# A one-core encoder block with 32 routed experts: how the first expert gets its rows, and when the half blocks add their lower part

## The chip, the cores and the metric

One core of one Trainium2 chip runs the whole layer in one launch. The metric is device time in microseconds (us), the median of several executions. Names: PE is the tensor engine, ACT the scalar engine, DVE the vector engine, POOL the GpSimd engine, SP the engine that here only issues DMAs.

## The reference

One layer over 1024 tokens of width 1024: a token mixer, a layer norm, a mixture of experts, a second layer norm. What matters here is the mixture; each token takes 2 of 32 experts, and each expert has three matrices of 2 MB.

```
x = layer_norm(ALPHA * x + mix, ln1_g, ln1_b)
gl = xf @ w_rg + b_rg                       # 4 groups, top 1
el = (xf @ w_re + b_re).reshape(T, 4, 8)    # 8 experts in the group, top 2
weights = (g_w[:, None] * top_v).reshape(-1)
hb = silu(xb @ w_gate[e]) * (xb @ w_up[e])  # per block of rows of one expert
yb = hb @ w_down[e]
y  = segment_sum(yb * row_w[:, None], row_tok)
x  = layer_norm(ALPHA * x + y, ln2_g, ln2_b)
```

The counts per expert are known only at run time.

## The kernel before, in words

**Numbers.** Every product is made of two-part splits: ACT copies a tile rounded (`hi`), DVE subtracts it from the tile (`lo`), and PE adds three products (`mm3`, lines 95 to 98). For expert weights this is `w_split`, lines 1005 to 1014: tiles `we` (raw), `weh` and `wel`.

**The end of the mixer.** A loop over 8 tiles of 128 tokens makes the output projection (`out_proj`, tiles `z`), `residual(i)` (DVE: sum, statistics), `r_transposed` and `logits` (PE), `route_a` (DVE: top 1 and top 2, one-hot rows `ahot`), `norm1` (ACT, then POOL in two passes, lines 844 and 845) and `store1`, which writes the normed rows to `x1d` in HBM. `rank` counts on PE how many earlier tokens chose each expert; `route_b` makes of it each token's place in a table `tabd` in HBM and scatters (token, weight) there with two indirect DMAs from POOL (line 939). Tile 7 comes last and alone.

**The start of the experts.** SP reads back the table's rows of the four first experts (`slots`, line 1082), and POOL gathers the rows of `x1d` that they name (`gather`, line 1193, tile `xin`). The first four experts (`FIXED`) are taken in their own order, the other 28 by falling count: lines 1085 to 1104 rank them on DVE with 28 x 28 comparisons on every partition and write `perm`, from which SP reads each expert's number.

**The expert stage.** An expert is six chunks of 1 MB: gate 0 and 1, up 2 and 3, down 4 and 5. `SEQ` has the order: chunks 0 to 3 of a block, then chunks 4 and 5 of the block before. SP issues the loads (`load_to`) as far ahead as 20 tiles in rotation allow; ACT and DVE split three chunks ahead (`AHEAD`); SP's queue also reads each later block's table rows (`place`, line 1188, tile `psl`, eight in rotation). Each block ends in an indirect DMA that adds its rows to `accd` in HBM (`finish`, line 1289).

**Half blocks.** Eleven of the 33 blocks have 64 rows (`few_rows`). They put both parts of the rows side by side, so PE needs two products in place of three; the second half of the partitions must then be added to the first. ACT copies it out (`low_part`, `low_y`, tiles `low` and `lowy`), and PE adds it with a product by the identity (`add_low`, line 1178). In the loop at line 1329 the gate's lower part is added after chunk 2, the down product's after the next chunk, which is the next block's chunk 0.

**Overflow.** `overflow_setup` (line 1117) works out which rows did not fit; some 30 DVE instructions at block 21.

Of the kernel before, what the change touches and what calls it, by code (L numbers as in the profile page):

```python
# [11 lines left out]
F32 = mybir.dt.float32  # L12
# [9 lines left out]
S = 1024  # L22
# [27 lines left out]
def kernel(  # L50
# [726 lines left out]
    lgc = rp_.tile([128, 2, 36], F32, name="lgc")  # L777
    wg = rp_.tile([128, KT, 36], F32, name="wg")

    def logit_setup():  # L780
# [75 lines left out]
    def store_acc(i):  # L856
        sp.dma_start(accd[i * 128:(i + 1) * 128], ACC[i])
# [19 lines left out]
    def route_a(i):  # L877
# [31 lines left out]
        a = rp_.tile([128, 2, NG, EPG], F32, name="ah", bufs=2)  # L909
# [10 lines left out]
    def rank(i):  # L920
# [5 lines left out]
        pe.matmul(rk, tri[:, 0, :], ahot[:, i, :], start=False, stop=True)  # L926
        RT[i] = rk, RT[i]

    def route_b(i):
        rk, av = RT[i]  # L930
        idf = rp_.tile([128, 2], F32, name="idf")
# [3 lines left out]
        idx = rp_.tile([128, 2], I32, name="idx", bufs=4)  # L935
        dve.tensor_copy(idx, idf)
        for c in range(2):
            pool.memset(spacer, 0.0)
            st = pool.indirect_dma_start(
                out=tabd, out_offset=bass.IndirectOffsetOnAxis(ap=idx[:, c:c + 1], axis=0),  # L940
                in_=pay[:, i, c, :], in_offset=None)
# [4 lines left out]
    SCAT = []  # L946
    spacer = rp_.tile([1, 1], F32, name="spacer")

# [84 lines left out]
    for i in range(NT):  # L1033
        if i + 1 < NT:
            load_xr(i + 1)
        load_to({0: 6, 2: 7, 5: 8, 6: 9, 7: 11}.get(i, 0))
        ka, kb = (K0, K0) if i == 0 else (2, 4) if i + 1 < NT else KLAST
        out_proj(i, 0, ka)
        if i:
            r_transposed(i - 1)  # L1040
        if i + 1 < NT:
            m_split(i + 1)
        if i > 1:
            store1(i - 2)
            scale_acc(i - 2)
            store_acc(i - 2)
        out_proj(i, ka, kb)
        if i:
            logits(i - 1)
            route_a(i - 1)  # L1050
        if i:
            norm1(i - 1)
        out_proj(i, kb, KT)
        if i == 0:
            logit_setup()
        if i:
# [5 lines left out]
    r_transposed(NT - 1)
    store1(NT - 2)
    scale_acc(NT - 2)
    store_acc(NT - 2)
    load_to(L2)
    norm1(NT - 1)
    logits(NT - 1)
    route_a(NT - 1)
    rank(NT - 1)  # L1070
    route_b(NT - 1)
    store1(NT - 1)


    tabv = tabd.rearrange("(r e) c -> r e c", e=NE)
    AHEAD = 3
    w_split(LOADS[0])
    scale_acc(NT - 1)
    for q in range(1, AHEAD):
        w_split(LOADS[q], low=False)  # L1080
    slots = const.tile([128, FIXED, 2], I32, name="slots")
    sp.dma_start(slots, tabv[0:128, 0:FIXED, :])
    store_acc(NT - 1)
    load_to(L3)
    cn = rpp.tile([128, NE], F32, name="cn", tag="lp", bufs=1)
    for t in range(NT):
        pe.matmul(cn, tri[:, 1, :], ahot[:, t, :], start=(t == 0), stop=(t == NT - 1))
# [6 lines left out]
    sq = [128, NV, NV]  # L1094
    key = rp_.tile([128, NV], F32, name="key")
    dve.tensor_add(key, cnf[:, FIXED:], ordc[:, 0:NV])
    osq = rp_.tile(sq, F32, name="osq", tag="r", bufs=3)
    dve.tensor_tensor(osq, key[:, None, :].to_broadcast(sq), key[:, :, None].to_broadcast(sq), op=ALU.is_gt)
    dve.tensor_reduce(rk28, osq, axis=AX.X, op=ALU.add)
    dve.tensor_tensor(osq, rk28[:, None, :].to_broadcast(sq), ordc[:, 2 * NV:, None].to_broadcast(sq),  # L1100
                      op=ALU.is_equal)
    dve.tensor_mul(osq, osq, ordc[:, None, NV:2 * NV].to_broadcast(sq))
    dve.tensor_reduce(key, osq, axis=AX.X, op=ALU.add)
    dve.tensor_copy(perm, key)
    w_split(LOADS[1], high=False)
# [9 lines left out]
    def overflow_setup():  # L1115

        rk = rk28
        cap = mp.tile([128, NE], F32, name="cap", bufs=1)
        pool.memset(cap[:, :FIXED], float(NE * ROWS[0]))
        pool.memset(cap[:, FIXED:], float(CAPS[-1] // CAP_UNIT))  # L1120
        for q, d in [(q, CAPS[q - 1] - CAPS[q]) for q in range(1, NV)] + [(1, ROWS["v"])]:
            for _ in range(d // CAP_UNIT):
                dve.scalar_tensor_tensor(cap[:, FIXED:], rk, float(q), cap[:, FIXED:], op0=ALU.is_lt, op1=ALU.add)
# [66 lines left out]
    def gather(b):  # L1190
        n = ROWS[b]
        XIN[b] = mp.tile([128, D], F32, name="xin", bufs=GA)
        pool.indirect_dma_start(out=XIN[b][:n], out_offset=None, in_=x1d,  # L1193
                                in_offset=bass.IndirectOffsetOnAxis(ap=IDX[b][:n, 0:1], axis=0))

    def x_transpose(b):
        n = ROWS[b]
# [40 lines left out]
                        (wh[:, k, HALF[half]], wl[:, k, HALF[half]]), kk == 0, kk == 3)  # L1238

    def low_part(b, t):  # L1240
        LOW[b, t] = mp.tile([64, DE], F32R, name="low", tag="h", bufs=1)
        take_low(LOW[b, t], GU[b, t])

    def gated(b):
# [48 lines left out]
    LATE = (3, 4)  # L1293
    for q in range(2):
        place(*BLOCKS[q])
        gather(BLOCKS[q][0])
    load_to(L4, pool)
    x_transpose(0)
    w_split(LOADS[2], high=False)
    load_to(NBIG + len(ASIDE) - AHEAD, pool)  # L1300

    NB = len(BLOCKS)
    ORD = {b: q for q, (b, p) in enumerate(BLOCKS)}
# [25 lines left out]
    waiting = []  # L1329
    for t, (b, p, c) in enumerate(SEQ):  # L1330
        if c not in LATE:
            run_ahead(t)
        chunk(b, p, c)
        if waiting:
            add_y(waiting[0])
            finish(waiting.pop())
        o = ORD[b]
        nxt = [u[0] for u in BLOCKS[o + 1:o + 1 + GA]] + [None] * GA
        if few_rows(b):
            if c in (1, 3):  # L1340
                low_part(b, c // 2)
            if c == 2:
                add_low(GU[b, 0], LOW[b, 0])
                gated(b)
        if c == 3:
# [205 lines left out]
```

## Time and profile before

| what | value |
|---|---|
| median of 3 runs | 1259.84 us (1259.83 to 1260.31) |
| the profiled execution | 1256.64 us, 3.2 below that median |
| its span, first to last instruction | 1254.7 us |
| TensorE clock granted, mean | 0.969 |
| busy: PE, DVE, ACT, POOL | 92%, 72%, 58%, 22% |
| HBM read, written | 252.32 MB, 25.97 MB |

The page shows the whole span in 40 slices of 31 us. The experts run from about 634 us to 1214 us, the end of the mixer before them from 500 us on. Times in the rows are from the span's start. A row of a timeline gives start, duration, engine, line, operation, what it writes and reads and, in brackets, how long the engine was idle before and what ended that.

### The profile page before, as it was taken

The page shows a single profiled execution, that of the slowest core. Times are in us where ns is not written, and L with a number is a line of the kernel's source. Part 1 is how long each engine was busy: PE and PEld are TensorE (multiplying, and loading weights), DVE is VectorE, ACT ScalarE, POOL GpSimd, SP SyncE. Part 2 cuts the span into 40 slices and gives each one's busy share as a digit, 9 for nine tenths or more (in the row PEclk, how much of TensorE's full clock was granted, in tenths as well). Part 3 has the DMA queues.
Part 4 walks back from the last instruction along what each step waited for, and adds up shares of the span by engine and source line. Part 5 has one row for each costly group of instructions (what it writes and reads, how often), then busy time and mean ns, then how long its engine had stood idle before and what let it go on. Part 6 is the DMA issues. An engine that isn't in the chain of part 4 may idle for free.

```text
span 1254.7 us, 16032 instructions
## 1 busy us (share of the span) xinstructions
PE 1151.4 (92%) x5630; PEld 873.4 (70%) x5630; DVE 899.4 (72%) x1274; ACT 732.7 (58%) x989; POOL 274.1 (22%) x213
## 2 busy tenths in 40 slices
PE   8999999999999998999389999999999979999970
PEld 7888778888888886877268767766756646656630
DVE  5688962222752237799878989898967988988857
ACT  5578772111231112432358888888867868897745
POOL 2322200000000003565542122221222212221110
PEclk9999999999999999999689999999999989999995
DMA  8000104111121126637589999999999999999956
GB/s 271 1 2 1 45 17 122 51 51 43 34 76 51 51 104 207 226 116 239 197 308 333 363 378 386 375 371 379 361 322 387 342 385 379 360 380 378 389 182 244
DMA packets 146766, 279.35 MB, mean 223 GB/s; under 512 B 18957, under 2 KB 50701, under 8 KB 146685
## 3 DMA queue, kind: packets, MB, share of 16 engines
q1 hardware_dynamic: 137453, 249.00, 54.6%
q0 software_dynamic: 9232, 29.32, 8.8%
q8 instruction: 45, 0.74, 0.2%
q14 instruction: 36, 0.29, 0.1%
HBM read 252.32 MB, written 25.97 MB: 222 GB/s over the span
## 4 chain that ended last, share of the span: by engine, by line
PE 72%; DVE 10%; ACT 8%; DMA 5%; issue 4%; POOL 1%; SPq 0%; DVEq 0%; POOLq 0%; ACTq 0%
PE gps L98 5%; PE gps L96 5%; PE gps L97 5%; ACT weh L1012 5%; PE yp L96 3%; PE gate L97 3%; PE gate L98 3%; PE gate L96 3%; PE up L97 3%; PE up L96 3%; PE up L98 3%; PE yp L98 3%; PE yp L97 3%; PE yps L97 2%; PE yps L98 2%
## 5 line engine op out<-in xcount | busy, mean ns | idle before, releaser
L1014 DVE TENSOR_TENSOR wel<-we,weh 128x2048 fp32r<-128x2048 f32 (+1 forms) x193 | 426.7, 2244 | 63.3 <-ACT weh L1012 62.1
L1012 ACT ACTIVATE weh<-we 128x2048 fp32r<-128x2048 f32 (+1 forms) x193 | 355.4, 1876 | 14.6 <-PE gate L97 5.5
L1289 POOL DMA_INDIRECT accd<-y,psl x29 | 68.3, 2357 | 370.2 <-ACT y L1288 284.5
L646 ACT ACTIVATE sig<-gps,bch 128x512 f32<-128x512 f32 x29 | 19.9, 687 | 169.1 <-PE gps L98 169.1
L98 PE MATMUL gps<-xh,ghl 128*128 128x512 f32 x296 | 115.3, 390 | 0.0
L96 PE MATMUL gps<-xh,ghl 128*128 128x512 f32 x296 | 115.2, 389 | 0.0
L97 PE MATMUL gps<-xl,ghl 128*128 128x512 f32 x296 | 115.2, 389 | 0.0
L92 DVE TENSOR_TENSOR ghl<-wraw,ghl 128x1024 fp32r<-128x1024 f32 (+1 forms) x26 | 26.4, 1020 | 82.4 <-ACT ghl L91 82.4
L96 PE MATMUL yp<-weh,hT 128*128 128x512 f32 (+7 forms) x176 | 72.5, 412 | 0.1
L97 PE MATMUL gate<-wel,xinT 128*128 128x512 f32 (+7 forms) x176 | 69.5, 395 | 2.3 <-DVE wel L1014 2.3
L96 PE MATMUL gate<-weh,xinT 128*128 128x512 f32 (+7 forms) x176 | 69.9, 397 | 0.8 <-ACT xinT L91 0.8
L98 PE MATMUL gate<-weh,xinT 128*128 128x512 f32 (+7 forms) x176 | 69.1, 393 | 0.2 <-DVE xinT L92 0.2
L98 PE MATMUL yp<-weh,hT 128*128 128x512 f32 (+7 forms) x176 | 69.1, 392 | 0.0
L97 PE MATMUL yp<-wel,hT 128*128 128x512 f32 (+7 forms) x176 | 69.0, 392 | 0.0
L96 PE MATMUL up<-weh,xinT 128*128 128x512 f32 (+7 forms) x176 | 69.0, 392 | 0.0
L97 PE MATMUL up<-wel,xinT 128*128 128x512 f32 (+7 forms) x176 | 68.9, 391 | 0.0
L98 PE MATMUL up<-weh,xinT 128*128 128x512 f32 (+7 forms) x176 | 68.9, 391 | 0.0
L96 PEld LDWEIGHTS gps<-xh,ghl 128*128 128x128 f32 x296 | 55.6, 188 | 11.7
L97 PEld LDWEIGHTS gps<-xl,ghl 128*128 128x128 f32 x296 | 55.6, 188 | 11.7
L98 PEld LDWEIGHTS gps<-xh,ghl 128*128 128x128 f32 x296 | 55.6, 188 | 11.6
L91 ACT ACTIVATE xinT<-xtp 128x256 fp32r<-128x256 f32 (+8 forms) x66 | 27.5, 465 | 59.2 <-PE xtp L1203 58.9
L1193 POOL DMA_INDIRECT xin<-x1d,psl x29 | 53.8, 1856 | 16.1 <-DMA psl<-tabd 7.6
(312 smaller groups left out, 2691.6 us busy)
## 6 DMA issues: line engine op xcount, KB each, us to landing
we<-in_w_gate_dram SPq DMA_DIRECT2D x62, 1024.0 KB, 14.3
we<-in_w_up_dram SPq DMA_DIRECT2D x61, 1024.0 KB, 14.0
we<-in_w_down_dram SPq DMA_DIRECT2D x60, 1024.0 KB, 14.4
wraw<-in_w_in_dram SPq DMA_DIRECT2D x20, 512.0 KB, 4.1
x<-in_x_dram SPq DMA_DIRECT2D x8, 512.0 KB, 9.7
wo<-in_w_o_dram SPq DMA_DIRECT2D x4, 1024.0 KB, 6.3
xr<-in_x_dram SPq DMA_DIRECT2D x8, 512.0 KB, 3.5
x1d<-r SPq DMA_DIRECT2D x8, 512.0 KB, 4.4
```

Of the source, the lines that this page charges most:

```text
L91: act.activation(hi, src, AF.Copy)
L92: dve.tensor_sub(lo, src, f(hi))
L96: pe.matmul(ps, lh, rh, start=first, stop=False)
L97: pe.matmul(ps, lh, rl, start=False, stop=False)
L98: pe.matmul(ps, ll, rh, start=False, stop=last)
L646: act.activation(dst[:, HALF[half]], ps, fn, bias=bch[:, bcol:bcol + 1])
L1012: act.activation(hi[:, sl], raw, AF.Copy)
L1014: dve.tensor_sub(lo[:, sl], raw, f(hi[:, sl]))
L1193: pool.indirect_dma_start(out=XIN[b][:n], out_offset=None, in_=x1d, in_offset=bass.IndirectOffsetOnAxis(ap=IDX[b][:n, 0:1], axis=0))
L1289: pool.indirect_dma_start(out=accd, out_offset=bass.IndirectOffsetOnAxis(ap=IDX[b][:n, 0:1], axis=0), in_=y[:n], in_offset=None, compute_o ...
```

## The change

1. **Lower parts later.** A half block's gate part is added after chunk 3 in place of chunk 2 (its copy gets a tile of its own), the down product's part after the next block's chunk 1 in place of chunk 0; `gated` and `finish` of the half blocks move with them.
2. **Overflow spread.** `overflow_setup` becomes a generator: three small instructions or one larger one per block, from block 15 on.
3. **First expert's slots on chip.** Tile 7's places become one-hot rows, and two small products with constants turn them into the rows that the first expert needs from tile 7 (`slot0`). What tiles 0 to 6 put there is read from the table by one more DMA (`base0`) behind tile 6's scatter. The first gather takes `slot0`. Tile 7's scatter and the read of `slots` come behind that gather. A tiny POOL write and a DVE copy of it (`spacer`) keep DVE's next weight split behind the first gather's issue.
4. **Experts ordered one to a partition.** 28 x 28 comparisons on 28 partitions, with two products to spread the result.
5. **Around it.** Tiles 6 and 7 are normed by DVE (`norm1_dve`, two instructions) and not by ACT and POOL; ranking and scatter of tiles 0 to 5 move one tile later; their conversion to integers goes from DVE to POOL; the loads 16 to 20 go from POOL's queue to SP's.

```diff
+    def norm1_dve(i):
+        x1, mv = X1[i], MV1[i]
+        dve.scalar_tensor_tensor(x1, x1, mv[:, 0:1], ln_g, op0=ALU.subtract, op1=ALU.mult)
+        dve.scalar_tensor_tensor(x1, x1, mv[:, 2:3], ln_b, op0=ALU.mult, op1=ALU.add)
...
+    def places(i):
+        IDT[i] = idlast if i == NT - 1 else rp_.tile([128, 2], I32, name="idx", bufs=4)
+        if i < NT - 1:
+            pool.tensor_copy(IDT[i], IDF[i])
+            return
+        dve.tensor_scalar(hot0, iota, IDF[i][:, 0:1], None, op0=ALU.is_equal)
+        dve.scalar_tensor_tensor(hot0, iota, IDF[i][:, 1:2], hot0, op0=ALU.is_equal, op1=ALU.add)
+        dve.tensor_copy(IDT[i], IDF[i])
...
+        if i > 1:
+            rank(i - 2)
+            route_b(i - 2)
+            places(i - 2)
+            scatter(i - 2)
         out_proj(i, ka, kb)
...
-        out_proj(i, kb, KT)
+            (norm1_dve if last else norm1)(i - 1)
+        out_proj(i, kb, KT - 1 if last else KT)
-        if i:
+        if last:
             rank(i - 1)
             route_b(i - 1)
+            out_proj(i, KT - 1, KT)
         residual(i)
+        if last:
+            places(i - 1)
+            scatter(i - 1)
+            base0 = const.tile([128, 2], I32, name="base0")
+            sp.dma_start(base0, tabv[0:128, 0, :])
     L1, L2, L3, L4 = 14, 15, 15, 16
     load_to(L1)
     r_transposed(N1)
...
+    logits(N1)
+    norm1_dve(N1)
+    store1(N1)
     load_to(L2)
+    w_split(LOADS[0], low=False)
+    route_a(N1)
...
+    for a in range(2):
+        pe.matmul(ps0, hot0, pay0[:, a, :], start=(a == 0), stop=(a == 1))
+    dve.scalar_tensor_tensor(slf, ps0[:, 1:2], rcol[:, 3:4], base0[:, 0:1], op0=ALU.mult, op1=ALU.add)
+    dve.tensor_add(slot0, slf, ps0[:, 0:1])
...
-        gather(BLOCKS[q][0])
-    load_to(L4, pool)
+    gather(0)
+    pool.memset(spacer[:, 1:2], 0.0)
+    dve.tensor_copy(spacer[:, 0:1], spacer[:, 1:2])
+    w_split(LOADS[0], high=False)
+    scatter(N1)
+    load_to(NBIG + len(ASIDE) - AHEAD - 1)
+    sp.dma_start(slots, tabv[0:128, 0:FIXED, :])
+    gather(1)
     x_transpose(0)
-    w_split(LOADS[2], high=False)
-    load_to(NBIG + len(ASIDE) - AHEAD, pool)
+    for q in range(1, AHEAD):
+        w_split(LOADS[q], high=False)
+    load_to(NBIG + len(ASIDE) - AHEAD)
...
-        if waiting:
+        if waiting and c == 1:
             add_y(waiting[0])
             finish(waiting.pop())
...
-            if c == 2:
+            if c == 3:
                 add_low(GU[b, 0], LOW[b, 0])
                 gated(b)
...
-            if o == NB - 12:
-                overflow_setup()
+            if o >= NB - 18:
+                next(pieces, None)
```

SP's queue between the store of tile 5 and the first expert's tables, before:

```order
98 L848 DMA x1d<-r 128x1024
99 L857 DMA accd<-acc 128x1024
100 L1002 DMA we<-in_w_down_dram 128x2x1024 x2
101 L1002 DMA we<-in_w_gate_dram 128x4x512
102 L848 DMA x1d<-r 128x1024
103 L857 DMA accd<-acc 128x1024
104 L1002 DMA we<-in_w_gate_dram 128x4x512
105 L848 DMA x1d<-r 128x1024
106 L1082 DMA slots<-tabd 128x8
107 L857 DMA accd<-acc 128x1024
```

and in the change:

```order
100 L1104 DMA base_5416<-tabd 128x2
101 L1035 DMA we<-in_w_down_dram 128x2x1024 x2
102 L1035 DMA we<-in_w_gate_dram 128x4x512
103 L868 DMA x1d<-r 128x1024
104 L877 DMA accd<-acc 128x1024
105 L868 DMA x1d<-r 128x1024
106 L1035 DMA we<-in_w_gate_dram 128x4x512
107 L877 DMA accd<-acc 128x1024
```

The read of `base0`, which waits for tile 6's scatter, now stands ahead of three weight loads and of the last two stores to `x1d`. The read of `slots` no longer stands there; it follows on the same queue behind 4 MB of loads that POOL issued before:

```order
108 L1035 DMA we<-in_w_up_dram 128x4x512
109 L1035 DMA sg<-in_w_gate_dram 128x512
110 L1035 DMA h<-in_w_gate_dram 128x512
111 L1035 DMA xin<-in_w_gate_dram 128x2x512
112 L1035 DMA hT<-in_w_up_dram 128x2x512 x2
113 L1035 DMA y<-in_w_gate_dram 128x2x512 x2
114 L1367 DMA slots<-tabd 128x8
```

These are the loads 16 to 19, four chunks (three of them into tiles that later hold `sg`, `h`, `xin`, `hT` and `y`), ahead of the read.

PE in the first half block, from the end of its gate product on, before:

```order
3094 L1168 MATMUL up<-weh,xinT 128x512
3095 L1169 MATMUL up<-wel,xinT 64x512
3096 L1178 MATMUL gate<-low,identr 64x512
3097 L1168 MATMUL up<-weh,xinT 128x512
3098 L1169 MATMUL up<-wel,xinT 64x512
3099 L1168 MATMUL up<-weh,xinT 128x512
3100 L1169 MATMUL up<-wel,xinT 64x512
3101 L1168 MATMUL up<-weh,xinT 128x512
3102 L1169 MATMUL up<-wel,xinT 64x512 x2
3103 L1171 MATMUL up<-weh,xinT 128x512
3104 L1203 MATMUL xtp<-ident,xin 128x128 x8
3105 L1178 MATMUL up<-low,identr 64x512
```

and in the change:

```order
3120 L1232 MATMUL up<-weh,xinT 128x512
3121 L1233 MATMUL up<-wel,xinT 64x512
3122 L1232 MATMUL up<-weh,xinT 128x512
3123 L1233 MATMUL up<-wel,xinT 64x512
3124 L1232 MATMUL up<-weh,xinT 128x512
3125 L1233 MATMUL up<-wel,xinT 64x512 x2
3126 L1235 MATMUL up<-weh,xinT 128x512
3127 L1242 MATMUL gate<-low,identr 64x512
3128 L1267 MATMUL xtp<-ident,xin 128x128 x8
3129 L1242 MATMUL up<-low,identr 64x512
```

The gate's addition moves from the middle of the up product to its end; the addition for the up product stays.

## Rows read from the trace of the kernel before

**Rows 1.** Stretches: us, busy us of PE, PEld, DVE, ACT, POOL; clock; DMA share; GB/s.
```profile
620.00:630.00 10.00, 0.00 (x0) 0.00 (x0) 7.71 (x10) 2.55 (x3) 5.89 (x5) 0.50 0.21 63
640.00:670.00 30.00, 29.02 (x139) 23.69 (x138) 26.99 (x22) 24.50 (x25) 3.98 (x4) 1.00 0.88 308
920.00:930.00 10.00, 10.00 (x45) 7.25 (x44) 6.10 (x6) 6.81 (x7) 1.31 (x1) 1.00 0.76 266
1100.00:1200.00 100.00, 97.27 (x457) 58.94 (x456) 87.65 (x58) 83.94 (x79) 21.06 (x9) 1.00 1.04 387
...
1200.00:1220.00 20.00, 14.18 (x63) 6.95 (x61) 8.68 (x10) 5.85 (x8) 2.93 (x3) 0.97 0.33 84
```

**Rows 2.** Timeline, from the last tile's sum to the first expert's first product.
```profile
592.52 0.93 SPq L1002 DMA_DIRECT2D we<-in_w_down_dram  x2
...
601.30 1.77 DVE L936 CAST idx<-idf 128x2 int32<-128x2 f32 x1
602.99 1.27 DVE L825 SCALAR_TENSOR_TENSOR r<-xr,z 128x512 f32<-128x512 f32 x2
...
607.85 1.24 ACT L839 ACTIVATE r<-r,mv 128x1024 f32<-128x1024 f32 x1 [0.86 <-DVE mv L832]
...
608.85 0.26 DVE L880 SCALAR_TENSOR_TENSOR lg<-lp,mv,lt 128x36 f32<-128x36 f32 x1 [0.75 <-PE lp L873]
...
611.75 2.20 DVE L893 TENSOR_SCALAR ro<-ro,rw 128x4 f32<-128x4 f32 x1
...
613.94 0.32 SPq L848 DMA_DIRECT2D x1d<-r  x1
...
618.00 3.05 POOL L939 DMA_INDIRECT tabd<-pay,idx  x1 [4.03 <-DVE idx L936]
...
623.57 0.33 SPq L1082 DMA_DIRECT2D slots<-tabd  x1
...
625.72 2.28 DVE L1014 TENSOR_TENSOR wel<-we,weh 128x2048 fp32r<-128x2048 f32 x1
626.00 2.87 POOL L1193 DMA_INDIRECT xin<-x1d,slots  x1 [3.59 <-DMA slots<-tabd]
629.17 0.95 POOL L1193 DMA_INDIRECT xin<-x1d,slots  x1 [0.30 <-issue]
...
632.24 1.97 PE L1203 MATMUL xtp<-ident,xin 128*128 128x128 f32 x8 [14.85 <-DMA xin<-x1d,slots]
...
634.04 0.80 PE L96 MATMUL gate<-weh,xinT 128*128 128x512 f32 x1
...
645.62 1.03 PE L1203 MATMUL xtp<-ident,xin 128*128 128x128 f32 x8
```

**Rows 3.** Timeline: the same DVE operation on 128x1024 in the final norm.
```profile
1228.30 2.43 DVE L1450 SCALAR_TENSOR_TENSOR r<-r,mv,ln_gb 128x1024 f32<-128x1024 f32 x2
```

**Rows 4.** Waits of PE, 640 to 1220 us: total, times, longest.
```profile
PE gate L1178 <- ACT low L1175: 8.4, 9, 1.2
PE gate L1169 <- DVE wel L1014: 6.2, 3, 5.7
PE yp L1178 <- ACT lowy L1175: 4.3, 5, 1.2
```

**Rows 5.** Timeline: DVE's overflow instructions.
```profile
1009.86 4.41 DVE L1123 SCALAR_TENSOR_TENSOR cap<-rk,cap 128x28 f32<-128x28 f32 x20
```

**Rows 6.** Waits of ACT, then of SP's queue, in the expert stage.
```profile
ACT weh L1012 <- DMA we<-in_w_down_dram: 0.8, 1, 0.8
...
SPq L1188 <- DMA accd<-y,psl: 83.2, 13, 9.5
```

**Rows 7.** DMA issues, 670 to 1195 us: count, KB each, us from issue to landing.
```profile
we<-in_w_gate_dram SPq DMA_DIRECT2D x54, 1024.0 KB, 15.1
...
xin<-x1d,psl POOLq DMA_INDIRECT x28, 8.8
...
psl<-tabd SPq DMA_DIRECT2D x9, 0.5 KB, 13.6
```

More of the change, by code (lines that the diff above doesn't have):

```diff
@@ L778 @@
     wg = rp_.tile([128, KT, 36], F32, name="wg")
+    iota = rp_.tile([128, 128], BF, name="iota")
+    rcol = const.tile([128, 4], F32, name="rcol")
+    pay0 = rp_.tile([128, 2, 2], BF, name="pay0")
+    hot0 = rp_.tile([128, 128], BF, name="hot0")
     def logit_setup():
@@ L792, in logit_setup @@
         dve.tensor_add(lgc[:, 1], ps[:, 1], br)
+        pi = rpp.tile([128, 128], F32, name="iotap", tag="rk", bufs=1)
+        pe.matmul(pi, tri[:, 1, :], tri[:, 0, :], start=True, stop=True)
+        dve.tensor_scalar(iota, pi, 1.0 / 32, None, op0=ALU.mult)
+        pool.memset(pay0, 0.0)
+        pool.memset(pay0[:, 0, 1:2], 1.0)
+        pool.memset(pay0[:, 1, 0:1], float(128 * (NT - 1) - S))
+        dve.tensor_scalar(rcol[:, 3:4], crow, -1.0 / 32, float(S), op0=ALU.mult, op1=ALU.add)
+        dve.tensor_scalar(pay0[:, 0, 0:1], rcol[:, 3:4], -1.0, None, op0=ALU.mult)
+        dve.tensor_scalar(rcol[:, 0:1], crow, -1.0 / 32, float(NV - 1 + S), op0=ALU.mult, op1=ALU.add)
+        dve.tensor_scalar(rcol[:, 1:2], crow, 1.0 / 32, float(FIXED - S), op0=ALU.mult, op1=ALU.add)
     def rstd_of(r, v, t):
@@ L908, in route_a @@
         first(sel, v[5], rev8, c8, v[6], hot[:, 1])
-        a = rp_.tile([128, 2, NG, EPG], F32, name="ah", bufs=2)
+        a = rp_.tile([128, 2, NG, EPG], F32, name="ah", bufs=3)
         ash = [128, 2, NG, EPG]
@@ L927, in rank @@
         RT[i] = rk, RT[i]
+    SCAT, IDF, IDT = [], {}, {}
+    spacer = const.tile([1, 2], F32, name="spacer")
+    idlast = const.tile([128, 2], I32, name="idlast")
+    tabv = tabd.rearrange("(r e) c -> r e c", e=NE)
     def route_b(i):
         rk, av = RT[i]
-        idf = rp_.tile([128, 2], F32, name="idf")
+        idf = IDF[i] = rp_.tile([128, 2], F32, name="idf", bufs=3)
         for c in range(2):
@@ L934, in route_b, with scatter @@
                                      accum_out=idf[:, c:c + 1])
-        idx = rp_.tile([128, 2], I32, name="idx", bufs=4)
-        dve.tensor_copy(idx, idf)
+    def places(i):
[6 more added lines that the diff above has]
+        dve.tensor_copy(IDT[i], IDF[i])
+    def scatter(i):
         for c in range(2):
-            pool.memset(spacer, 0.0)
+            pool.memset(spacer[:, 0:1], 0.0)
             st = pool.indirect_dma_start(
-                out=tabd, out_offset=bass.IndirectOffsetOnAxis(ap=idx[:, c:c + 1], axis=0),
+                out=tabd, out_offset=bass.IndirectOffsetOnAxis(ap=IDT[i][:, c:c + 1], axis=0),
                 in_=pay[:, i, c, :], in_offset=None)
@@ L944, in route_b @@
             SCAT.append(st)
-    SCAT = []
-    spacer = rp_.tile([1, 1], F32, name="spacer")
     WIDE = sum(c > 64 for c in CAPS)
@@ L1046 @@
             store_acc(i - 2)
+        if i > 1:
[3 more added lines that the diff above has]
+            scatter(i - 2)
         out_proj(i, ka, kb)
+        last = i == NT - 1
         if i:
@@ L1050 @@
             route_a(i - 1)
-        if i:
-            norm1(i - 1)
-        out_proj(i, kb, KT)
+            (norm1_dve if last else norm1)(i - 1)
+        out_proj(i, kb, KT - 1 if last else KT)
         if i == 0:
             logit_setup()
-        if i:
+        if last:
             rank(i - 1)
             route_b(i - 1)
+            out_proj(i, KT - 1, KT)
         residual(i)
+        if last:
[3 more added lines that the diff above has]
+            sp.dma_start(base0, tabv[0:128, 0, :])
@@ L1060 @@
     L1, L2, L3, L4 = 14, 15, 15, 16
+    AHEAD = 3
+    N1 = NT - 1
     load_to(L1)
[L1062 to L1065, printed above, removed]
-    load_to(L2)
[L1067 to L1078, printed above, removed]
+    r_transposed(N1)
+    store1(N1 - 1)
+    scale_acc(N1 - 1)
+    store_acc(N1 - 1)
@@ L1079 @@
+    logits(N1)
+    norm1_dve(N1)
+    store1(N1)
+    load_to(L2)
+    w_split(LOADS[0], low=False)
+    route_a(N1)
+    scale_acc(N1)
+    store_acc(N1)
     for q in range(1, AHEAD):
         w_split(LOADS[q], low=False)
+    rank(N1)
     slots = const.tile([128, FIXED, 2], I32, name="slots")
-    sp.dma_start(slots, tabv[0:128, 0:FIXED, :])
-    store_acc(NT - 1)
-    load_to(L3)
+    route_b(N1)
+    places(N1)
+    ps0 = rpp.tile([128, 2], F32, name="slp", tag="x1Tp", bufs=2)
+    for a in range(2):
+        pe.matmul(ps0, hot0, pay0[:, a, :], start=(a == 0), stop=(a == 1))
@@ L1085 @@
+    slot0 = const.tile([128, 1], I32, name="slot0")
+    slf = const.tile([128, 1], F32, name="slf")
+    dve.scalar_tensor_tensor(slf, ps0[:, 1:2], rcol[:, 3:4], base0[:, 0:1], op0=ALU.mult, op1=ALU.add)
+    dve.tensor_add(slot0, slf, ps0[:, 0:1])
     cn = rpp.tile([128, NE], F32, name="cn", tag="lp", bufs=1)
     for t in range(NT):
-        pe.matmul(cn, tri[:, 1, :], ahot[:, t, :], start=(t == 0), stop=(t == NT - 1))
+        pe.matmul(cn, tri[:, 1, :], ahot[:, t, :], start=(t == 0), stop=(t == N1))
@@ L1088 @@
+    cc = rpp.tile([NV, 1], F32, name="cc", tag="x1Tp", bufs=2)
+    for t in range(NT):
+        pe.matmul(cc, ahot[:, t, FIXED:], tri[:, 1, 0:1], start=(t == 0), stop=(t == N1))
     cnf = const.tile([128, NE], F32, name="cnf")
@@ L1092 @@
     novi = const.tile([128, 1], I32, name="novi")
[L1094 to L1105, printed above, removed]
+    key = rp_.tile([NV, NV], F32, name="key", tag="em")
+    keyc = rp_.tile([NV, 2], F32, name="keyc")
+    hotk = rp_.tile([NV, NV], F32, name="hotk", tag="lg")
+    rkb = rp_.tile([NV, 128], F32, name="rkb", tag="x1T")
+    dve.tensor_add(key, cnf[:NV, FIXED:], ordc[:NV, 0:NV])
+    dve.tensor_add(keyc[:, 0:1], cc, rcol[:NV, 0:1])
+    dve.tensor_scalar(key, key, keyc[:, 0:1], None, op0=ALU.is_gt)
+    dve.tensor_reduce(keyc[:, 1:2], key, axis=AX.X, op=ALU.add)
+    dve.tensor_scalar(hotk, ordc[:NV, 2 * NV:], keyc[:, 1:2], None, op0=ALU.is_equal)
+    dve.tensor_copy(rkb, keyc[:, 1:2].to_broadcast([NV, 128]))
+    pp = [rpp.tile([128, NV], F32, name="z", tag="z", bufs=4) for _ in range(2)]
+    pe.matmul(pp[0][0:1], rcol[:NV, 1:2], hotk, start=True, stop=True)
+    pe.matmul(pp[1], rkb, ident[:NV, :NV], start=True, stop=True)
+    dve.tensor_copy(perm[0:1], pp[0][0:1])
+    dve.tensor_copy(rk28, pp[1])
     pc.close()
@@ L1120, in overflow_setup @@
         pool.memset(cap[:, FIXED:], float(CAPS[-1] // CAP_UNIT))
-        for q, d in [(q, CAPS[q - 1] - CAPS[q]) for q in range(1, NV)] + [(1, ROWS["v"])]:
-            for _ in range(d // CAP_UNIT):
-                dve.scalar_tensor_tensor(cap[:, FIXED:], rk, float(q), cap[:, FIXED:], op0=ALU.is_lt, op1=ALU.add)
+        steps = [q for q, d in [(q, CAPS[q - 1] - CAPS[q]) for q in range(1, NV)] + [(1, ROWS["v"])]
+                 for _ in range(d // CAP_UNIT)]
+        for n, q in enumerate(steps):
+            dve.scalar_tensor_tensor(cap[:, FIXED:], rk, float(q), cap[:, FIXED:], op0=ALU.is_lt, op1=ALU.add)
+            if n % 3 == 2:
+                yield
         dve.tensor_scalar(cap[:, FIXED:], cap[:, FIXED:], float(NE * CAP_UNIT), None, op0=ALU.mult)
@@ L1127, in overflow_setup @@
         sh = [128, 8, NE]
+        yield
         dve.tensor_add(ovc, ovc, cap[:, None, :].to_broadcast(sh))
+        yield
         val = mp.tile(sh, F32, name="val", bufs=1)
         dve.tensor_tensor(val, ovc, ct[:, None, :].to_broadcast(sh), op=ALU.is_lt)
+        yield
         pos = mp.tile([128, 8 * NE], F32, name="pos", bufs=1)
@@ L1133, in overflow_setup @@
         dve.tensor_tensor_scan(pos, vflat, vflat, 0.0, op0=ALU.add, op1=ALU.bypass)
+        yield
         dve.tensor_copy(novi, pos[:, 8 * NE - 1:])
@@ L1193, in gather @@
         pool.indirect_dma_start(out=XIN[b][:n], out_offset=None, in_=x1d,
-                                in_offset=bass.IndirectOffsetOnAxis(ap=IDX[b][:n, 0:1], axis=0))
+                                in_offset=bass.IndirectOffsetOnAxis(ap=slot0 if b == 0 else IDX[b][:n, 0:1], axis=0))
     def x_transpose(b):
@@ L1240, in low_part @@
     def low_part(b, t):
-        LOW[b, t] = mp.tile([64, DE], F32R, name="low", tag="h", bufs=1)
+        LOW[b, t] = mp.tile([64, DE], F32R, name="low", tag=("sg", "h")[t], bufs=1)
         take_low(LOW[b, t], GU[b, t])
@@ L1327, in run_ahead @@
                     [max(SPLIT[t] + NEAR, FULL)]))
-    waiting = []
+    waiting, pieces = [], overflow_setup()
     for t, (b, p, c) in enumerate(SEQ):
@@ L1373 @@
                 finish(b)
+    assert next(pieces, 0) == 0
     ln_gb2 = bigtile([128, 2, D], F32, "ln_gb2")
```

## The prediction

> **What bounds the kernel now.** Three views were read: stretches, the timeline of the slow stretch, then the waits. In the stretches [rows 1] PE is busy 97 of 100 us with experts, and nothing at all in 620 to 630. So two things matter: the hole between mixer and experts, and what paces the experts.
>
> The hole is one chain [rows 2]. The last tile's sum starts at 602.99 behind a conversion of 1.77 us on DVE; statistics take until 607.85; ACT and POOL norm the tile, and its store is issued at 613.94. Beside that DVE routes the tile, with steps like the one of 2.20 us at 611.75. POOL scatters the places from 618.00, SP reads the slots at 623.57, POOL gathers from 626.00, the rows are there at 632.24, PE's first product runs at 634.04.
>
> In the experts PE waits little: 8.4 and 4.3 us for the half blocks' lower parts and 6.2 for splits, 5.7 of it in one piece [rows 4], behind DVE's overflow instructions (the first 20 take 4.41 us) [rows 5]. That is 8.4 + 4.3 + 5.7 = 18.4 us which the change can take. But the DMA engines' share there is 1.04 almost throughout (the last 100 us stand in [rows 1] as one row): the transfers are as full as PE. A share below 1.04 stands only in the first 30 us (0.88), where loads must wait for free tiles, and in 920 to 930 (0.76). ACT waits for a load once, 0.8 us [rows 6], so loads still arrive in time, just.
>
> **The change part by part, against the profiled execution (1256.64).**
>
> *Last tile's sum.* The conversion leaves DVE (1.77 us, for POOL, beside other work). Tile 6's norm comes to DVE: two instructions of about 1.22 us (half of 2.43) [rows 3], while PE still multiplies. PE also waited a little for late sums in earlier tiles. I take the sum of tile 7 at 599.5, 3.5 us earlier; between 1.5 and 4.
>
> *Store.* Statistics need 607.85 - 602.99 = 4.9 us as before; DVE's two norm steps follow, 2.5 us, in place of ACT and POOL. Issue at about 607, against 613.94.
>
> *Slots.* Routing now comes behind the norm on DVE, at 607. It took 618.00 - 608.85, about 9 us [rows 2], of which the step at 611.75 alone, 2.20 for four elements a row, is 2 us too long beside POOL's passes. These are gone; I take 5 (at most 7). The one-hot rows, two small products and two additions cost about 2 more (estimate, ten or so steps of 0.2). `slot0` is ready at 614. What disappears is the scatter, the table's read and the wait for both, 618.00 to 626.00. The ordering of experts shrinks from 784 elements a step to 28; it lay beside this chain and gives nothing by itself.
>
> *The new wait.* The first gather also needs the last store landed. SP issues `base0` first and holds for tile 6's scatter. Two scatters with their landing took 623.57 - 618.00 = 5.6, less the 2 by which the first (3.05) was long: 3.6, so from 599.5 to about 603.5. Behind it stand three loads of 1 MB that went out from 592.52 before [rows 2], two half-MB stores, then the store in question. A small read on SP's queue lands 13.6 us after issue where loads stand ahead of it [rows 7], almost as a load does (15.1), so this queue serves in order. 4.2 MB at 308 to 387 GB/s [rows 1] are 11 to 14 us; with its own 0.5 MB the store lands at 616 to 619. I take 617: the gather waits 3 us for it, not for the slots.
>
> *Gather.* Issue took 2.87 us, the next 0.95 [rows 2]. The first ran beside a DVE split (625.72, 2.28 us), the second beside none. The change keeps the split back, so I take 0.95. After issue the rows needed 632.24 - 628.87 = 3.4 us on idle transfers; under loads issue to landing is 8.8 [rows 7]. Loads now run beside it, so I take 7.5: rows at 624.5 (ends 621 and 628). First product 1.8 later: 626.3, against 634.04: **7.7 gained**. The split kept back, 2.3 us from 618, is done before the rows arrive.
>
> [...]
>
> *Second expert.* Its gather needs tile 7's scatter and `slots`, which now stand on SP's queue behind the loads (about 6 MB after the store, until 632 or so). Its rows land at 638 to 640; PE is through the first block, 645.62 - 634.04 = 11.6 us [rows 2], at 638. **1 lost** (0 to 4).
>
> *Experts.* The half blocks' additions come a chunk later, about 2 us of PE work, more than the longest wait of 1.2 [rows 4]; the overflow pieces, at most 0.7 us, fit between DVE's splits. So PE's 18.4 us are gone if nothing else paces. But transfers at 1.04 cannot be sped up. The stream of loads gains the hole at 920, (1.04 - 0.76) x 10 / 1.04 = 2.7 us, and no more. Behind the last loads, PE runs on to 1214 (14.18 us busy after 1200, DMA share 0.33) [rows 1]: a part of that, at most some 5 us, is backlog that a faster PE would have done. I take 2.7 + 3.3 = **6 gained**; ends 2 and 18.4. It lies nearer to the low end because of the 0.8 us that ACT already waits.
>
> *Sum.* -7.7 + 1 - 6 = -12.7: 1243.9 for the profiled execution. The median of the runs stands 3.2 above that one, so 1247.
>
> **The rivals.**
> *PE keeps all 18.4.* For it: no wait on loads but 0.8 us. Against: the share. -7.7 + 1 - 18.4 = -25.1, 1235.
> *The transfers take all.* The experts gain nothing, as each us that PE saves turns into a wait of ACT on a load: -6.7, 1253.
> *The slots were not the last wait.* If the store lands only at 626, where the gather stood before, the whole part on the first expert is empty, and the half blocks' 6 stay: 1254.
> *Slower: SP's queue runs dry.* SP reads the tables of later blocks, and those reads wait for the additions to `accd` of earlier blocks: 83.2 us in 13 waits, the longest 9.5 [rows 6]. Eleven half blocks now finish a chunk, up to 2.7 us, later. This costs nothing while loads issued before still run, 15.1 us of them [rows 7]; it decides where SP is held longer than that. The one hole at 920 says this happens now and then. Were each of the eleven to empty the queue by 2.7 us, 30 would be lost: -6.7 + 30 = +23, 1283.
>
> **How the numbers follow.** The forecast has 0.53; PE keeping all 0.12; the transfers taking all 0.20; an empty first part 0.07; slower 0.05; 0.03 for none of these. A measurement of this kernel can tell 0.2%, 2.5 us, from no change. Forecast, PE's full gain and most of the cases at 1253 and 1254 are faster by more: 0.90. Same 0.05, slower 0.05. For the range: the forecast's own ends are rows at 621 with 10 us of the experts (-11 + 0 - 10 = -21, 1239) and a store at 619, rows at 628, 4 us lost at the second expert, 2 gained (-4.2 + 4 - 2 = -2, 1258). Both ends at once are unlikely; 1237 to 1256 takes in the two middle rivals and leaves out PE's full gain and the slower case.
>
> **What would show it.** Right: the last store issued near 607 and landing after `slot0` is written; the first gather at about 617, its issue near 1 us; first product near 626; PE's waits for `low` and `lowy` gone; no stretch of 4.41 us of `cap` instructions; ACT waiting on loads for several us in place of 0.8, with the DMA share at 1.04 also in 920 to 930. Wrong: a gather that starts before the store's queue is through, or after 622; PE's waits gone and no new wait of ACT on loads (then all 18.4 come); DMA shares well below 1.04 beside long waits of SP on `accd` (then slower).

## The result and the profile after

The changed kernel takes 1266.51 us (median of 5, 1264.49 to 1267.33) against 1259.83 (1256.26 to 1260.31): ratio 1.0058, 95% interval 1.0046 to 1.0071. That is 6.7 us slower, where 1247.0 was forecast, and above the range. The profiled execution takes 1265.1, its span is 1263.3, the mean granted clock 0.965 (0.969 before).

The start of the experts came almost as forecast. Timeline of the changed kernel, the rows that answer to [rows 2]:

```profile
598.26 1.28 DVE L840 SCALAR_TENSOR_TENSOR r<-xr,z 128x512 f32<-128x512 f32 x2
...
602.27 0.33 SPq L1104 DMA_DIRECT2D base<-tabd  x1
602.69 0.90 SPq L1035 DMA_DIRECT2D we<-in_w_down_dram  x2
603.68 0.42 SPq L1035 DMA_DIRECT2D we<-in_w_gate_dram  x1
...
605.91 0.32 SPq L868 DMA_DIRECT2D x1d<-r  x1
...
611.80 0.15 DVE L1135 TENSOR_TENSOR slot<-slf,slp 128x1 int32<-128x1 f32 x1
...
618.87 0.98 POOL L1257 DMA_INDIRECT xin<-x1d,slot  x1 [17.77 <-DMA x1d<-r]
...
620.04 2.27 DVE L1047 TENSOR_TENSOR wel<-we,weh 128x2048 fp32r<-128x2048 f32 x1
...
620.91 2.27 POOL L975 DMA_INDIRECT tabd<-pay,idlast  x1 [0.65 <-issue]
...
623.49 0.97 POOL L975 DMA_INDIRECT tabd<-pay,idlast  x1 [0.23 <-issue]
...
627.10 1.94 PE L1267 MATMUL xtp<-ident,xin 128*128 128x128 f32 x8 [13.17 <-DMA xin<-x1d,slot]
...
628.92 0.80 PE L96 MATMUL gate<-weh,xinT 128*128 128x512 f32 x1
```

The first product comes at 628.92 in place of 634.04, 5.1 us earlier. The gather was released by the last store (`x1d`), 7 us after `slot0` was ready. Block 1 starts 4.7 us earlier, and at 850 us the kernel is 6.4 us ahead (block 13 at 849.89, before at 856.33). The loss comes later: the last block starts at 1199.34, 8.3 us behind the kernel before. Stretches as in [rows 1]; the last column is what the transfers moved. First one of the kernel before that [rows 1] lacks:

```profile
590.00:600.00 10.00, 10.00 (x55) 8.60 (x55) 7.12 (x37) 3.88 (x7) 4.77 (x6) 1.00 0.85 297
```

The changed kernel:

```profile
core 0: us, PE busy (x) PEld busy (x) DVE busy (x) ACT busy (x) POOL busy (x), PEclk, DMA share, GB/s
590.00:600.00 10.00, 9.35 (x55) 7.29 (x54) 8.42 (x32) 0.94 (x4) 3.30 (x7) 1.00 0.14 53
...
640.00:670.00 30.00, 29.12 (x139) 23.67 (x139) 26.61 (x22) 24.92 (x24) 8.01 (x4) 1.00 0.80 253
920.00:930.00 10.00, 10.00 (x50) 7.33 (x48) 6.05 (x9) 7.25 (x10) 0.61 (x1) 1.00 0.93 310
...
1100.00:1200.00 100.00, 91.78 (x435) 56.09 (x434) 82.67 (x57) 78.40 (x72) 19.44 (x8) 1.00 1.05 372
```

In 590 to 600 the transfers stand nearly still, as three loads now wait behind `base0` (DMA share 0.14, before 0.85); 640 to 670 has 0.80 in place of 0.88, and the hole of 920 to 930 is mostly filled, 0.93 in place of 0.76 [rows 1]. In the last 100 us the DMA engines are as full as before (1.05, before 1.04), yet they move 372 GB/s in place of 387 [rows 1]. The waits between 640 and 1220 us (engine, line, tile, releaser: total us, times, longest) say who pays:

```profile
ACT weh L1045 <- DMA we<-in_w_down_dram: 17.0, 22, 3.5
...
ACT weh L1045 <- DMA we<-in_w_up_dram: 9.6, 14, 1.1
ACT weh L1045 <- DMA we<-in_w_gate_dram: 8.2, 8, 1.8
...
PE gate L1233 <- DVE wel L1047: 6.5, 6, 1.8
PE up L1233 <- DVE wel L1047: 6.0, 8, 1.8
PE gate L97 <- DVE wel L1047: 5.9, 8, 1.9
...
PE yp L1242 <- ACT lowy L1239: 3.9, 1, 3.9
PE up L1242 <- ACT low L1239: 3.2, 4, 1.2
PE gate L1242 <- ACT low L1239: 1.4, 1, 1.4
```

ACT waits 17.0 + 9.6 + 8.2 = 34.8 us for loads where it waited 0.8 [rows 6]. PE's waits for the lower parts of gate and down have shrunk from 8.4 + 4.3 [rows 4] to one each, 1.4 and 3.9; those of up have grown from 0.4 to 3.2. In their place it waits for splits, 6.5 + 6.0 + 5.9 us, where it waited 8.5 in all. On SP's queue, the time from the issue of the 28th load to the last issue (the second half of the 192nd) is 516.6 us before and 532.0 after: 15.4 us more, for the same bytes. Below this is called the stream; the expectations name its ends load 24 and load 192.

Why a full queue moves less is seen in single packets. The DMA view of 1000 to 1180 us gives for the queue of the loads its packets, MB and share of 16 engines. Before:

```profile
q1 hardware_dynamic: 26592, 62.06, 90.8%
```

The same row of the changed kernel:

```profile
q1 hardware_dynamic: 26097, 60.09, 90.9%
```

0.908 x 180 x 16 / 62.06 = 42.1 us of one engine for a MB before, 0.909 x 180 x 16 / 60.09 = 43.6 after: 3.4% more. The median packet of 2048 bytes took 84 ns before and 87 to 88 after, one of 4096 bytes 159 and 164. The difference, 1.43 us / 16 for each of the stream's 172 MB, makes 15.4 us: the whole loss of the stream. The question for the experiments is what slows a packet.

One thing differs that the diff doesn't say. The constant tiles lie below the 20 rotating weight tiles in SBUF, and the change adds six small ones (`rcol`, `spacer`, `idlast`, `base0`, `slot0`, `slf`) of 32 bytes each as placed. So all weight tiles start 192 bytes higher in every partition: at 21440 in place of 21248 for the first, the others at steps of 8192. 21248 is a multiple of 256 (83 x 256), 21440 is not. What else lies above the constants (the splits, the gathered rows, the results) moves with them.

### The profile page after: what moved, and what is told of

It reads as the page before. It is cut to its first block, busy times and chain, and to the rows that moved or that the text cites. A ratio compares the mean times of both kernels' runs of the same rounds, so it can differ in the third digit from the quotient of the medians.

```text
span 1263.3 us, 16035 instructions
## 1 busy us (share of the span) xinstructions
PE 1157.6 (92%) x5645; PEld 874.3 (69%) x5645; DVE 880.2 (70%) x1282; ACT 734.4 (58%) x987; POOL 264.9 (21%) x211
## 4 chain that ended last, share of the span: by engine, by line
PE 69%; DMA 14%; DVE 8%; ACT 5%; issue 3%; SPq 0%; POOL 0%; DVEq 0%; POOLq 0%; ACTq 0%
PE gps L98 5%; PE gps L96 5%; PE gps L97 5%; DMA we<-in_w_up_dram 5%; DVE wel L1047 3%; DMA we<-in_w_gate_dram 3%; ACT weh L1045 3%; PE gate L97 3%; PE yp L96 3%; PE gate L98 3%; PE z L96 2%; PE gate L96 2%; DMA we<-in_w_down_dram 2%; PE yp L98 2%; PE yp L97 2%
## 5 line engine op out<-in xcount | busy, mean ns | idle before, releaser
L1257 POOL DMA_INDIRECT xin<-x1d,psl x29 | 61.4, 2118 | 15.3 <-DVE wel L1047 6.7
L96 PE MATMUL z<-woh,mhl 128*128 128x512 f32 x128 | 52.7, 411 | 4.3 <-DVE sig L668 4.3
```

Of the source, the lines that this page charges most:

```text
L96: pe.matmul(ps, lh, rh, start=first, stop=False)
```

## Experiments

The runs were made in three batches, each with the kernel before beside it (1259.44, 1259.34 and 1258.46 us). Ratios are to that one; differences in us between batches, as 1266.51 to 1248.28, are good to about 1 us.

**The address alone.** Four kernels ran with one unused constant tile each, two of them the kernel before and two the changed one. The edit, here with 192 bytes:

```diff
     ident = const.tile([128, 128], F32, name="ident")
+    pad = const.tile([128, 48], F32, name="pad")
```

> The kernel before with one unused constant tile of 192 bytes a partition, so that the 20 weight tiles start at 21440 in each partition (as they do after the change) and not at 21248; no instruction differs. Theory 'address': the change lost its time because its new constant tiles moved the weight tiles by 192 bytes, to addresses that are no multiple of 128 or 256, and each packet of 2048 bytes is written there some 3% slower. Then this kernel's packets take 87 to 88 ns in place of 84, the stream of loads from load 24 to load 192 takes about 532 us in place of 517, ACT begins to wait for loads, and the time rises by 8 to 15 us: 1268 to 1275. Rival 'order': packets are slower because of what the change put side by side (a faster PE, loads 16 to 20 on SP's queue). Then nothing moves here: 1257 to 1261, packets 84 ns. Rival 'chip': the changed kernel was profiled on a slower chip or at a worse moment. Then packets may be at 87 here too, but the ratio to the kernel before on this same chip is 1.000.

> The changed kernel with one unused constant tile of 64 bytes, so that the weight tiles start at 21504, a multiple of 1024. Theory 'address': packets of 2048 bytes at 84 ns again, the stream 15 us shorter, and the time comes to about what the prediction's steps give without it: 1245 to 1255, faster than the kernel before. Rivals 'order' and 'chip': 1264 to 1268 as the changed kernel, packets 87 to 88 ns.

> The changed kernel with 320 unused bytes: weight tiles at 21760, which is a multiple of 256 and of no more, the same class as in the kernel before (21248). Theory 'address': like the run with 64 bytes, 1245 to 1255; if a multiple of 512 mattered, 2 us or more slower than that one. Rivals: 1264 to 1268.

> The kernel before with 256 unused bytes: weight tiles at 21504, a multiple of 1024, in place of a multiple of 256. Theory 'address', if 256 is enough: no change, 1257 to 1261. If more alignment still helps, packets of under 84 ns and up to 10 us less. Rival 'order': no change.

| kernel | weight tiles at | past a multiple of 256 | us | ratio to before, 95% |
|---|---|---|---|---|
| before, +192 | 21440 | 192 | 1273.97 | 1.0116 (1.0100 to 1.0131) |
| changed, +64 | 21504 | 0 | 1248.28 | 0.9918 (0.9904 to 0.9931) |
| changed, +320 | 21760 | 0 | 1250.40 | 0.9933 (0.9920 to 0.9947) |
| before, +256 | 21504 | 0 | 1258.57 | 0.9991 (0.9982 to 1.0000) |

The kernel before (1259.44 beside these runs) becomes 14.5 us slower without one instruction changed, and the changed kernel 18.2 us faster (1266.51 to 1248.28; by the ratios, 1.0058 to 0.9918, 17.6). 'Order' and 'chip' both fall. In the kernel before with 192 bytes more, packets of 2048 bytes take 88 ns and ACT waits 14.6 us for loads. The page's account of the load queue over the whole span, in the kernel before:

```profile
q1 hardware_dynamic: 137453, 249.00, 54.6%
```

and with 192 bytes more, for the same packets:

```profile
q1 hardware_dynamic: 137453, 249.00, 55.2%
```

That is 0.552 x 1272.5 = 702 us of all engines against 0.546 x 1254.7 = 685. Its stream takes 530.3 us. The changed kernel at 21504, 1000 to 1180 us:

```profile
q1 hardware_dynamic: 27285, 63.45, 92.0%
```

0.920 x 180 x 16 / 63.45 = 41.8 us a MB, as fast as before; packets of 84 ns again; the stream takes 515.2 us. A multiple of 1024 gives at most 2 us more than one of 256 alone (1248.28 and 1250.40, with intervals that overlap). These runs move everything above the constants, so the place of the weight tiles was not tried by itself; that the loads' packets are slower is seen.

**How far past.** Two more places for the changed kernel, 192 and 96 unused bytes; by the theory '256' both are as slow as the changed kernel itself:

> The changed kernel with 192 unused bytes: weight tiles at 21632, 128 past a multiple of 256. Theory '256': a packet of 2048 bytes costs more as soon as its place in a partition is no multiple of 256, so this is as slow as the changed kernel itself (21440, 192 past): packets of 87 to 88 ns, stream 530 to 532 us, time 1262 to 1268. Rival '128 or 64 is enough': packets 84 ns, 1247 to 1251. Rival 'only SBUF sharing with some other tile': neither the one nor the other number.

> The changed kernel with 96 unused bytes: weight tiles at 21536, 32 past a multiple of 256 and of 1024. [...] Rival 'each 32 bytes past cost': less than for 192 past, packets of 84.5 to 85, 1250 to 1254. Rival '64 is what matters, and less is worse': over 88 ns and over 1268.

128 past: 1264.52, ratio 1.0054 (1.0039 to 1.0069). 32 past: 1266.77, ratio 1.0063 (1.0047 to 1.0078). The changed kernel as it is, 192 past, has 1.0058. Packets of 2048 bytes take 87 to 88 ns in all three; the streams of the two runs take 528.6 and 533.4 us, just outside the 530 to 532 expected. So at these three places it is a step and not a slope: on a multiple of 256, or not. The runs agree with a price for each packet that does not grow with the distance (3 to 4 ns of 84, 5 of 159 at 4096 bytes); what in a packet takes that time is not shown.

**What parts 1 and 2 are worth.** On the changed kernel at 21504:

```diff
-        LOW[b, t] = mp.tile([64, DE], F32R, name="low", tag=("sg", "h")[t], bufs=1)
+        LOW[b, t] = mp.tile([64, DE], F32R, name="low", tag="h", bufs=1)
...
-        if waiting and c == 1:
+        if waiting:
...
-            if c == 3:
+            if c == 2:
                 add_low(GU[b, 0], LOW[b, 0])
...
-            if o >= NB - 18:
-                next(pieces, None)
+            if o == NB - 12:
+                for _ in pieces:
+                    pass
```

> The changed kernel with weight tiles at 21504, and its parts 1 and 2 undone: lower parts added after chunk 2 and after the next block's chunk 0 as before, all of the overflow work at one block. What is left of the change is the start of the experts. Theory 'transfers': from about 1000 us on the stream of loads sets the pace in both, so the two parts are worth 1 to 3 us: 1249 to 1251. Rival 'PE': PE's 18.4 us of waits come back, half of them at least: 1257 to 1267. Rival 'harm': the parts cost something when loads are late, because ACT's copy of the lower part stands behind a split that waits for a load: 1244 to 1247.

1252.71, ratio 0.9951 (0.9937 to 0.9964): the two parts are worth 4.4 us, between the first two theories and clearly no harm. Waits of ACT on loads, with the two parts undone:

```profile
ACT weh L1046 <- DMA we<-in_w_up_dram: 0.6, 1, 0.6
ACT weh L1046 <- DMA we<-in_w_down_dram: 0.2, 1, 0.2
```

and with them (both at 21504):

```profile
ACT weh L1046 <- DMA we<-in_w_gate_dram: 7.4, 7, 3.0
ACT weh L1046 <- DMA we<-in_w_down_dram: 5.6, 11, 1.1
ACT weh L1046 <- DMA we<-in_w_up_dram: 5.0, 7, 1.2
```

Undone, PE sets the pace and loads are in time; with them PE is faster and 18.0 us of waits on loads appear. They look like what the transfers kept back. The next runs test that.

**Transfers with slack.** Three kernels that leave out the addition: a block's rows are written to `accd` and not added to what lies there:

```diff
-                                in_=y[:n], in_offset=None, compute_op=ALU.add)
+                                in_=y[:n], in_offset=None)
```

> The kernel before with weight tiles at 21504, in which each block writes its rows to accd where it should add them to what lies there: the last step's input is another, the order of all work is the same. A row of 4 KB that is added takes 260 to 278 ns of a DMA engine, one that is only written 159 to 173, so some 4000 of these free 4000 x 100 ns / 16 = 25 us of the transfers' time. Theory 'PE bounds the kernel before, transfers are only just as full': 0 to 3 us faster than the 1258.6 with additions. Rival 'transfers bound it already': 5 to 25 us faster.

> The same edit in the changed kernel with weight tiles at 21504. Theory 'transfers took what PE would have gained': with 25 us of slack in the transfers, ACT's 18 us of waits on loads vanish and PE keeps most of its 18.4: 5 to 10 us faster than the 1248.3 with additions, so 15 to 20 us faster than the kernel before under the same edit (10 with additions). Rival 'parts 1 and 2 are worth 4.4 whatever the transfers do': 1246 to 1248.

> The same edit in the changed kernel as it is, weight tiles at 21440. Theory 'address, by the transfers': packets still take 87 to 88 ns, but 3% of 515 us (15 us) is less than the 25 us freed, so the address costs next to nothing now: within 3 us of the run with weight tiles at 21504, where with additions it was 18 us. Rival 'the address also slows ACT, DVE or PE, which read these tiles': 10 to 18 us slower than that run here too.

(The 260 to 278 ns of the expectation is a mean over added rows and gathered ones; an added row alone has a median of 327, a written one 159. Over all indirect packets the edit frees 28.8 us of all 16 engines in the kernel before and 29.6 in the changed one, not 25.) Kernel before at 21504: 1257.19, ratio 0.9991 (0.9980 to 1.0002), the same as with additions. Changed kernel at 21504: 1240.61, 7.7 us less. Changed kernel at 21440: 1245.39. ACT's waits on loads in the changed kernel at 21504:

```profile
ACT weh L1046 <- DMA we<-in_w_down_dram: 1.8, 4, 0.6
ACT weh L1046 <- DMA we<-in_w_up_dram: 1.3, 3, 0.7
ACT weh L1046 <- DMA we<-in_w_gate_dram: 0.3, 1, 0.3
```

3.4 us in place of 18.0, and the lead over the kernel before under the same edit is 1257.19 - 1240.61 = 16.6 us in place of 10.3. So the kernel before was bound by PE, and in the changed one the transfers keep back about 6 us. It is not that SP waits less for rows to land in `accd`: in the changed kernel at 21504 those waits are 71.7 us with additions and 83.9 without. PE did not keep all 18.4 even here: from first product to the last `yp` it gains 580.1 - 571.3 = 8.8. Its waits for lower parts fall from 13.1 us (kernel before, same edit) to 2.0, but those for splits go from 8.8 to 10.2: spreading the overflow took away the one long wait, not their sum. The address costs 4.8 us here, not 18.2: more than the 3 that were expected, since PE's gain had used up part of the slack (ACT still waits 20.2 us on loads at 21440), and far less than the 10 to 18 expected of a slower ACT, DVE or PE. Nor is a split slower: ACT's takes 1912 ns and DVE's 2288 in the kernel before, 1912 and 2289 with 192 bytes more. So the address costs by way of the transfers.

**The store that the first gather waits for.** At 21504, the three loads put ahead of `base0` on SP's queue:

```diff
             places(i - 1)
             scatter(i - 1)
+            load_to(L1)
             base0 = const.tile([128, 2], I32, name="base0")
             sp.dma_start(base0, tabv[0:128, 0, :])
...
-    load_to(L1)
     r_transposed(N1)
```

> The changed kernel with weight tiles at 21504, and the three loads that stand on SP's queue behind the read of base0 put ahead of it. They then go out at about 589 to 594 and not at 602, when the transfers are at 0.14 of their time. Theory 'store': the first gather waits for the last store's landing (617.8, while slot0 is ready at 611), and that store stands behind these loads; so it lands at about 609, the gather starts at 611 to 612, the first product comes at 618 to 621 in place of 627, and since the transfers begin as much earlier the end moves with it: 1240 to 1245. Rival 'second expert': gather 1 still needs tile 7's scatter and the read of slots behind the loads, so block 1 starts at 639 to 641 as now and PE waits for it: 1246 to 1248. Rival 'buffers': the loads cannot go out before 600 either because their tiles are taken: no change, 1248.

1242.45, ratio 0.9879 (0.9864 to 0.9894): 5.8 us less than without, and 1.2% faster than the kernel before. Timeline:

```profile
588.34 1.26 SPq L1036 DMA_DIRECT2D we<-in_w_down_dram  x2
...
591.00 0.37 SPq L1036 DMA_DIRECT2D we<-in_w_gate_dram  x1
...
601.08 0.34 SPq L1106 DMA_DIRECT2D base<-tabd  x1
...
604.75 0.32 SPq L869 DMA_DIRECT2D x1d<-r  x1
...
610.63 0.16 DVE L1135 TENSOR_TENSOR slot<-slf,slp 128x1 int32<-128x1 f32 x1
611.06 0.99 POOL L1257 DMA_INDIRECT xin<-x1d,slot  x1 [11.13 <-DVE cnf L1144]
...
619.27 1.94 PE L1267 MATMUL xtp<-ident,xin 128*128 128x128 f32 x8 [6.37 <-DMA xin<-x1d,slot]
...
621.09 0.80 PE L97 MATMUL gate<-weh,xinT 128*128 128x512 f32 x1
```

The loads go out in the hole of 0.14; the store behind them no longer waits, the gather starts 0.3 us after `slot0` is written, and the first product comes at 621.09, 5.9 us before that of the same kernel without the edit (626.97). Block 1 follows at 634.70, 13.6 later. 'Store' holds, with its numbers; 'second expert' and 'buffers' fall.

## Why the prediction was wrong

*Last tile's sum* (599.5): 598.26. Right, a little better. *Store* (issue at 607): 605.91. *Slots* (ready at 614): 611.95, the end of the row at 611.80. One of the 2 us comes from the earlier norm and store, one from a shorter routing.

*The new wait* (store landed at 617, the last thing the gather waits for): the gather starts at 618.87 in the changed kernel and at 617.82 at 21504. Right, and for the reason given: the run with the loads put ahead takes exactly this wait away.

*Gather* (0.95 us of issue because no split runs beside it): 0.98. The scatter behind it, beside a split (620.04, 2.27 us), takes 2.27 and its second half, beside none, 0.97. Here as in [rows 2] the slow issue ends 0.87 us after the split does. Why an issue beside a split takes longer, no run here shows. *First product* (626.3, 7.7 gained): 628.92 in the changed kernel, 5.1 gained, as the gather started 1.9 later than forecast; 626.97 at 21504, 7.1 gained. The address doesn't make this difference: the changed kernel at 21760 has 629.47, those 128 and 32 past a multiple of 256 have 627.80 and 628.50.

*Second expert* (1 lost): block 1 starts 14.07 us after the first product at 21504 and 13.86 in the changed kernel, where it was 13.44. 0.4 to 0.6 lost, no more than the kernel before varies by itself (13.87 at 21504).

*Experts* (6 gained, since "transfers at 1.04 cannot be sped up"): 4.4, measured at 21504. The mechanism was the one named: the gain turned into ACT's waits on loads. PE had less to give than the 18.4 us that I added up: 8.8, as the runs with slack show.

These steps together give what the runs at 21504 show: 1258.57 to 1248.28, 10.3 us (against 1259.44, 11.2), where 12.7 were forecast. The forecast of 1247 was, to 1 to 3 us, the time of the changed kernel with its weight tiles on a multiple of 256 (1248.28 and 1250.40).

**The step that failed** is the one on the experts, and there one unspoken assumption: that a byte takes as long after the change as before. I wrote that the stream could gain 2.7 us "and no more", took its share of 1.04 as a fixed bound, and no rival made a byte slower (the slower one emptied the queue). No term of the sum priced the six small constant tiles. The term is +18.2 us in the changed kernel (1266.51 - 1248.28), and it turned a gain of some 11 us into a loss of 6.7. In the kernel before the same term alone is 14.5.

The slower rival, SP's queue run dry by `accd`, did not happen: SP's waits there fell from 83.2 us [rows 6] to 52.7 in 8, though the longest grew from 9.5 to 10.8. 'The transfers take all' came nearest in kind, ACT waiting on loads at a full share; but it held the transfers' end fixed, and could not give a loss.

A second thing had no price in the sum: what a wait of PE costs behind it. Block 16 of the changed kernel, timeline around its longest hole:

```profile
907.02 1.91 ACT L1045 ACTIVATE weh<-we 128x2048 fp32r<-128x2048 f32 x1 [3.49 <-DMA we<-in_w_down_dram]
...
908.03 0.40 PE L1235 MATMUL gate<-weh,xinT 128*128 128x512 f32 x1
...
909.75 1.91 ACT L1045 ACTIVATE weh<-we 128x2048 fp32r<-128x2048 f32 x1 [0.82 <-DMA we<-in_w_gate_dram]
911.68 1.08 ACT L1239 ACTIVATE lowy<-yp 64x512 fp32r<-64x512 f32 x2
...
912.33 1.17 PE L1242 MATMUL yp<-lowy,identr 64*64 64x512 f32 x2 [3.90 <-ACT lowy L1239]
...
913.42 0.79 PE L1232 MATMUL up<-weh,xinT 128*128 128x512 f32 x1
```

ACT waits 3.49 us for a late load, and the copy of the lower part (`lowy`) stands behind two such splits on ACT's queue. So the late load reaches PE by the very copy that the change had given a chunk of time. The stretches there (clock granted in the column PEclk):

```profile
908.00:912.00 4.00, 0.43 (x2) 0.00 (x0) 2.60 (x2) 3.16 (x3) 0.00 (x0) 0.89 1.05 385
912.00:916.00 4.00, 3.67 (x8) 2.13 (x9) 1.98 (x1) 2.61 (x5) 1.41 (x1) 0.50 1.06 382
916.00:920.00 4.00, 4.00 (x18) 2.52 (x18) 0.00 (x0) 0.51 (x1) 1.02 (x2) 0.76 1.08 372
```

In the 4 us in which PE starts again, after 3.9 without work, the granted clock is 0.50, in the next 4 it is 0.76; up to 917.8 a product takes 0.62 to 0.79 us, where it took 0.39 to 0.40. The block lasts 22.18 us, where the same block at 21504, without the hole, lasts 15.94: 6.2 us for a wait of 3.9. This block and the two before it cost 9.2 of the 16.4 us by which the changed kernel's last block starts behind that of the run at 21504.

## What to carry to other kernels

Where transfers are full, look up where the tiles that receive them start before and after any edit that adds even a small constant below them, and keep them on a multiple of 256 bytes, as at the three places that were fast here (21248, 21504, 21760) and none of the three slow ones (21440, 21536, 21632): a pad of 64 bytes was worth 18 us here, 4 times what the edits of the half blocks and the overflow work brought. Once a stream of loads is as full as PE, price what PE saves by what the stream lets through (here 4.4 us of the 18.4 added up), and test that by giving the transfers slack. And see what stands ahead, on its queue, of the one small store that a chain waits for: three loads issued 12 to 13 us earlier, in a hole of the transfers, were worth 5.8 us.

## What the runs showed of the hardware that was not expected

- A DMA packet of 2048 bytes into SBUF took 84 ns where the tile starts on a multiple of 256 bytes and 87 to 88 where it starts 32, 128 or 192 past one; 4096 bytes took 159 and 164. The DMA share doesn't show it (1000 to 1180 us: 1.04 before, 1.05 in the changed kernel); the GB/s and the packets' own times do.
- The same 192 bytes cost 14.5 us (kernel before), 18.2 (changed) and 4.8 (changed, with slack in the transfers): how much depends on whether the loads set the pace.
- A hole of 3.9 us in PE's work cost 6.2: the clock granted was 0.50 in the 4 us in which PE started again and 0.76 in the next 4.
- Two programs with the same instructions in the same order differ by 1.2% through the place of their tiles alone. Their pages show it in what the load queue takes for the same packets and bytes: 54.6% of 1254.7 us and 55.2% of 1272.5.
